# A row-sum kernel: both halves of a row summed at once in the last rows, loads of 9, 4 and 2 rows, and the first rows in two contiguous parts

**Chip and metric.** One core of a Trainium2 chip. The metric is the device time of one execution in microseconds (us); lower is better.

## The reference

```python
def setup_inputs():
    batch, seq, dim = 32, 512, 1024
    return {"x": np.random.randn(batch, seq, dim).astype(np.float32), "divisor": float(dim)}

def reference(x, divisor):
    return (np.sum(x, axis=-1) / divisor).astype(np.float32)
```

16384 rows of 1024 float32 are read (67.1 MB), 16384 numbers are written (64 KB). Each of the 128 partitions takes 128 rows.

## The kernel before

One queue (SP) issues every transfer. The first 16 rows of a partition lie in one part of the input, the other 112 in a second; each partition's results go out as 16, 96 and 16 neighbouring numbers, in three stores.

```python
F, L = 16, 16
M = J - F - L                      # 96
W = M + L                          # 112
x_first = bass.AP(tensor=x.tensor, offset=0, ap=[[F * D, P], [D, F], [1, D]])
... # x_main, x_last: pitch of W rows, behind x_first
o_first = bass.AP(tensor=out.tensor, offset=0, ap=[[F, P], [1, F]])      # 64 bytes a partition
o_main = bass.AP(tensor=out.tensor, offset=P * F, ap=[[W, P], [1, M]])
o_last = bass.AP(tensor=out.tensor, offset=P * F + M, ap=[[W, P], [1, L]])

first = [(2, 0), (14, 0)]          # (rows of a load, rows of it that ScalarE sums)
main = [(14, 0)] * 5 + [(14, 4), (12, 5)]
last = [(8, 4), (4, 2), (2, 1)]
...
    nc.vector.reduce_sum(out=dst[:, :d], in_=t[:, :d, :], axis=AX)       # VectorE's rows of a load
...
# the last two rows: one in a load of its own, one in three pieces pa, pb, pc
tc.keep_in_program_order(nc.sync.dma_start(out=o_first, in_=res0))       # behind the last load
tc.keep_in_program_order(nc.sync.dma_start(out=o_main, in_=res))
...
tc.keep_in_program_order(nc.sync.dma_start(out=o_last, in_=fin))
```

At the end of the program SP waits until every transfer but the last store has landed, and only then issues that last store (in the profile before, the others had landed by 157.87 and it was issued at 158.18). The kernel moves the store there itself:

```python
end.instructions = [
    with_sync(drain, on_wait=tuple(needs.values())),     # all earlier transfers landed
    with_sync(store, on_wait=(done,), on_update=(add,)), # then the store of fin
    *end.instructions[1:-1],
    with_sync(last, on_update=(sub,)),
]
```

Of the kernel before, what the change touches and what calls it, by code (L numbers as in the profile page):

```python
# [8 lines left out]

F32 = mybir.dt.float32  # L10
ADD = mybir.AluOpType.add
MULT = mybir.AluOpType.mult
COPY = mybir.ActivationFunctionType.Copy
AX = mybir.AxisListType.X
SP = mybir.EngineType.SP
# [52 lines left out]
def close_while_storing(nc, landed):  # L68


    body, end = nc.main_func.blocks[1], nc.main_func.blocks[-1]
    store = [i for i in body.instructions if i.engine == SP and type(i).__name__ == "InstDMACopy"][-1]
    (lane,) = store.sync_info.on_update
    drain = end.instructions[0]
    assert drain.engine == SP and type(drain).__name__ == "InstDrain"
    needs = {w.id: w for w in drain.sync_info.on_wait}
    assert needs[lane.id].wait_value > lane.update_value
    needs[lane.id] = dataclasses.replace(
        needs[lane.id], wait_value=needs[lane.id].wait_value - lane.update_value
    )  # L80

    (done,) = [w for w in store.sync_info.on_wait if w.ant_name.startswith("DVE_")]
    assert needs[done.id].wait_value == done.wait_value
    del needs[done.id]
    own = dict(sync_type="semaphore", id=landed.num, ant_name=landed.name)
    add = mybir.SyncUpdate(update_mode="sem-add-imm", update_value=16, **own)
    sub = mybir.SyncUpdate(update_mode="sem-sub-imm", update_value=16, **own)
    last = nc.sync.wait_ge(landed, 16).ins
    assert nc.main_func.blocks[-1].instructions[-1].name == last.name
    body.instructions = [i for i in body.instructions if i.name != store.name]  # L90
    end.instructions = [
        with_sync(drain, on_wait=tuple(needs.values())),
        with_sync(store, on_wait=(done,), on_update=(add,)),
        *end.instructions[1:-1],
        with_sync(last, on_update=(sub,)),
    ]


@with_exitstack
def kernel(  # L100
    ctx: ExitStack,
    tc: tile.TileContext,
    x: bass.AP,
    divisor: float,
    out: bass.AP,
):
    nc = tc.nc
    landed = nc.alloc_semaphore("landed")
    nc.at_finalize(start_loads_at_once)
    nc.at_finalize(latest_wait_first)  # L110
    nc.at_finalize(lambda nc: close_while_storing(nc, landed))
    xf = x.flatten_outer_dims()
    N, D = xf.shape
    P = nc.NUM_PARTITIONS
    scale = 1.0 / float(divisor)
    J = N // P
    assert J * P == N


    F, L = 16, 16  # L120
    M = J - F - L
    W = M + L
    x_first = bass.AP(tensor=x.tensor, offset=0, ap=[[F * D, P], [D, F], [1, D]])
    x_main = bass.AP(tensor=x.tensor, offset=P * F * D, ap=[[W * D, P], [D, M], [1, D]])
    x_last = bass.AP(tensor=x.tensor, offset=P * F * D + M * D, ap=[[W * D, P], [D, L], [1, D]])
    o_first = bass.AP(tensor=out.tensor, offset=0, ap=[[F, P], [1, F]])
    o_main = bass.AP(tensor=out.tensor, offset=P * F, ap=[[W, P], [1, M]])
    o_last = bass.AP(tensor=out.tensor, offset=P * F + M, ap=[[W, P], [1, L]])


    first = [(2, 0), (14, 0)]
    main = [(14, 0)] * 5 + [(14, 4), (12, 5)]
    last = [(8, 4), (4, 2), (2, 1)]
    assert sum(n for n, _ in first) == F
    assert sum(n for n, _ in main) == M and sum(n for n, _ in last) == L - 2
    bulk = ctx.enter_context(tc.tile_pool(name="bulk", bufs=3))
    one = ctx.enter_context(tc.tile_pool(name="one", bufs=1))
    psum = ctx.enter_context(tc.tile_pool(name="junk", bufs=4, space=bass.MemoryType.PSUM))

    res0 = one.tile([P, F], F32, name="res0")  # L140
    res = one.tile([P, M], F32, name="res")
    fin = one.tile([P, L], F32, name="fin")
    q = one.tile([P, L], F32, name="q")

    r = one.tile([P, 16], F32, name="r")[:, :1]

    def load(dst, src):
        tc.keep_in_program_order(nc.sync.dma_start(out=dst, in_=src))  # L148

    def act_sum(dst, src, by=1.0):  # L150
        n = src.shape[-1]
        junk = psum.tile([P, D], F32, name="junk")
        nc.scalar.activation(junk[:, :n], src, COPY, scale=by, accum_out=dst)  # L153

    def sums(dst, t, rows, on_act):
        d = rows - on_act
        for i in range(d, rows):
            act_sum(dst[:, i : i + 1], t[:, i, :])
        nc.vector.reduce_sum(out=dst[:, :d], in_=t[:, :d, :], axis=AX)  # L159

    for loads, src, dst in ((first, x_first, res0), (main, x_main, res)):
        j = 0
        for rows, on_act in loads:
            t = bulk.tile([P, 14, D], F32, name="t")
            load(t[:, :rows, :], src[:, j : j + rows, :])
            sums(dst[:, j : j + rows], t, rows, on_act)
            j += rows
        nc.gpsimd.tensor_scalar_mul(out=dst, in0=dst, scalar1=scale)  # L168
    j = 0
    for rows, on_act in last:  # L170
        if rows == 8:
            t = bulk.tile([P, 14, D], F32, name="t")[:, :8, :]
        else:
            t = one.tile([P, rows, D], F32, name=f"t{rows}")
        load(t, x_last[:, j : j + rows, :])
        sums(q[:, j : j + rows], t, rows, on_act)
        j += rows


    c = 704  # L180
    row = one.tile([P, D], F32, name="row")
    load(row, x_last[:, j, :])
    act_sum(r, row[:, c:], by=scale)
    nc.vector.reduce_sum(out=q[:, j : j + 1], in_=row[:, :c], axis=AX)  # L184



    a, b = 448, 704
    pa = one.tile([P, a], F32, name="pa")
    pb = one.tile([P, b - a], F32, name="pb")  # L190
    pc = one.tile([P, D - b + 2], F32, name="pc")
    load(pa, x_last[:, L - 1, :a])
    load(pb, x_last[:, L - 1, a:b])
    load(pc[:, : D - b], x_last[:, L - 1, b:])


    tc.keep_in_program_order(nc.sync.dma_start(out=o_first, in_=res0))
    tc.keep_in_program_order(nc.sync.dma_start(out=o_main, in_=res))

    act_sum(pc[:, D - b : D - b + 1], pa)  # L200
    nc.vector.reduce_sum(out=pc[:, D - b + 1 :], in_=pb, axis=AX)  # L201
    nc.gpsimd.tensor_scalar_mul(out=fin[:, :j], in0=q[:, :j], scalar1=scale)  # L202
    nc.gpsimd.tensor_scalar(  # L203
        out=fin[:, j : j + 1], in0=q[:, j : j + 1], scalar1=scale, scalar2=r, op0=MULT, op1=ADD
    )
    scaled = one.tile([P, D - b + 2], F32, name="scaled")
    nc.vector.tensor_scalar(  # L207
        out=scaled, in0=pc, scalar1=scale, scalar2=0.0, op0=MULT, op1=ADD, accum_out=fin[:, L - 1 :]
    )
    tc.keep_in_program_order(nc.sync.dma_start(out=o_last, in_=fin))  # L210


# [33 lines left out]
```

## Time and profile before

| | before |
|---|---|
| time, median of 5 runs | 161.13 us (160.92 to 161.52) |
| span of the profiled run | 159.6 us |
| VectorE busy | 120.9 us (76%) |
| DMA engines busy | 98.0% |
| last data landed / VectorE ended / last store issued | 157.54 / 158.15 / 158.18 us |

The kernel is bound by its stream of loads (the DMA engines are busy for 98.0% of the span, VectorE for 76%); the prediction shows the lines for that. The trace has 16 landing records, semaphore increments, for each of the 19 transfers, and a transfer is counted as landed at the last of them; a semaphore is the counter that others wait on. First the transfers of the results, with KB and the time from issue to landing, and then what SP waited for at the end (total, times, longest):

```profile
out_dram<-res SPq DMA_DIRECT2D x1, 48.0 KB, 10.1
out_dram<-res SPq DMA_DIRECT2D x1, 8.0 KB, 19.6
out_dram<-fin SPq DMA_DIRECT2D x1, 8.0 KB, 1.4
```
```profile
SPq L241 <- DMA out_dram<-res: 1.0, 1, 1.0
...
SPq L210 <- DVE scaled L207: 0.2, 1, 0.2
```

The first two stores were issued at 138.10 and 147.81 and landed at 157.70 and 157.87, just behind the last load (157.54). The line of 1.0 us covers the landing of the last pieces too. What SP waited for last was VectorE.

### The profile page before, as it was taken

Reading aid. Unit: us, or ns where it says so; the run is one execution under the profiler, and the core shown is the slowest. Engines: PE = TensorE matmul, PEld = TensorE weight load, DVE = VectorE, ACT = ScalarE, POOL = GpSimd, SP = SyncE. Lnnn points to the kernel's source line nnn. Section 1 sums busy time; section 2 is a strip of 40 time slices with the busy share of each in tenths; the row PEclk is TensorE's granted clock in tenths of the full one; section 3 lists DMA queues with packets and bytes.
Section 4 is the critical chain, followed back from the end, with each engine's and each line's share of the span. In section 5 each row is a group of like instructions: output and inputs, shape, how many; then the busy total and the mean of one; then the engine's idle time right before and its main releaser. Section 6 shows DMA issues by size and latency. Waiting matters only on the chain.

```text
span 159.6 us, 143 instructions
## 1 busy us (share of the span) xinstructions
DVE 120.9 (76%) x16; ACT 19.7 (12%) x37; POOL 1.4 (1%) x8
## 2 busy tenths in 40 slices
DVE  0500059995999599977999599959995996495985
ACT  3000000000000000000000000000000900490974
POOL 0000000000000000000000000000000000001001
DMA  7999999987999999978999999969999999898994
GB/s 253 470 460 460 460 460 460 431 374 345 460 460 460 460 460 460 417 345 388 460 460 460 460 460 460 402 302 445 460 460 427 394 431 542 357 443 378 413 407 133
DMA packets 2736, 67.18 MB, mean 421 GB/s; under 512 B 688, under 2 KB 1072, under 8 KB 1200
## 3 DMA queue, kind: packets, MB, share of 16 engines
q1 hardware_dynamic: 2736, 67.18, 98.0%
HBM read 67.11 MB, written 0.07 MB: 421 GB/s over the span
## 4 chain that ended last, share of the span: by engine, by line
DMA 76%; DVE 22%; SPq 0%; issue 0%; DVEq 0%
DMA t<-in_x_dram 76%; DVE res L159 20%; DVE q L159 1%; DVE q L184 1%; SPq L148 0%; DVE scaled L207 0%; DVE pc L201 0%; DVEq L207 0%; DVEq L241 0%
## 5 line engine op out<-in xcount | busy, mean ns | idle before, releaser
L159 DVE TENSOR_REDUCE res<-t 128x14 f32<-128x14336 f32 (+3 forms) x9 | 111.2, 12360 | 34.4 <-DMA t<-in_x_dram 34.4
L153 ACT ACTIVATE junk<-t 128x1024 f32<-128x1024 f32 x16 | 16.2, 1013 | 136.0 <-DMA t<-in_x_dram 136.0
L159 DVE TENSOR_REDUCE q<-t 128x4 f32<-128x4096 f32 (+2 forms) x3 | 7.9, 2642 | 2.7 <-DMA t<-in_x_dram 2.7
L153 ACT ACTIVATION_READ_ACCUMULATOR junk<-t 128x1 f32 x16 | 3.0, 187 | 0.0
L168 POOL TENSOR_SCALAR res<-res 128x16 f32<-128x16 f32 (+1 forms) x2 | 0.7, 352 | 145.1 <-DVE res L159 145.1
L153 ACT ACT_TABLE_LOAD x1 | 1.3, 1283 | 1.7 <-PEq L227 1.7
L184 DVE TENSOR_REDUCE q<-row 128x1 f32<-128x704 f32 x1 | 0.9, 885 | 0.0
L207 DVE TENSOR_SCALAR_CACHE_REDUCE scaled<-pc 128x322 f32<-128x322 f32 x1 | 0.5, 489 | 0.1
L153 ACT ACTIVATE junk<-pa 128x448 f32<-128x448 f32 x1 | 0.5, 547 | 0.0
L153 ACT ACTIVATE junk<-row 128x320 f32<-128x320 f32 x1 | 0.4, 442 | 0.1
L201 DVE TENSOR_REDUCE pc<-pb 128x1 f32<-128x256 f32 x1 | 0.4, 420 | 0.0
L202 POOL TENSOR_SCALAR fin<-q 128x14 f32<-128x14 f32 x1 | 0.3, 260 | 10.1 <-DVE q L159 10.1
L203 POOL TENSOR_SCALAR fin<-q,r 128x1 f32<-128x1 f32 x1 | 0.3, 265 | 0.7 <-DVE q L184 0.7
L153 ACT ACTIVATION_READ_ACCUMULATOR junk<-pa 128x1 f32 x1 | 0.2, 187 | 0.0
L153 ACT ACTIVATION_READ_ACCUMULATOR junk<-row 128x1 f32 x1 | 0.2, 186 | 0.0
L227 POOL MEMSET const-bfloat16-1.0<- 128x1 bf16 x1 | 0.1, 101 | 0.0
L227 POOL MEMSET const-uint8-127<- 128x1 uint8 x1 | 0.1, 101 | 0.0
L227 POOL MEMSET const-float32-0.0<- 128x1 f32 x1 | 0.1, 98 | 0.2 <-issue 0.2
L227 POOL MEMSET const-float32-1.0<- 128x1 f32 x1 | 0.1, 99 | 0.0
L207 DVE DVE_READ_ACCUMULATOR scaled<-pc 128x1 f32 x1 | 0.1, 82 | 0.0
## 6 DMA issues: line engine op xcount, KB each, us to landing
t<-in_x_dram SPq DMA_DIRECT2D x7, 7168.0 KB, 35.7
t<-in_x_dram SPq DMA_DIRECT2D x1, 6144.0 KB, 33.3
t<-in_x_dram SPq DMA_DIRECT2D x1, 4096.0 KB, 26.1
t<-in_x_dram SPq DMA_DIRECT2D x2, 1024.0 KB, 18.7
t<-in_x_dram SPq DMA_DIRECT2D x1, 2048.0 KB, 30.5
row<-in_x_dram SPq DMA_DIRECT2D x1, 512.0 KB, 33.2
pa<-in_x_dram SPq DMA_DIRECT2D x1, 224.0 KB, 33.3
pc<-in_x_dram SPq DMA_DIRECT2D x1, 160.0 KB, 33.0
```

The costliest lines, as they stand in the source:

```text
L153: nc.scalar.activation(junk[:, :n], src, COPY, scale=by, accum_out=dst)
L159: nc.vector.reduce_sum(out=dst[:, :d], in_=t[:, :d, :], axis=AX)
L168: nc.gpsimd.tensor_scalar_mul(out=dst, in0=dst, scalar1=scale)
L184: nc.vector.reduce_sum(out=q[:, j : j + 1], in_=row[:, :c], axis=AX)
L201: nc.vector.reduce_sum(out=pc[:, D - b + 1 :], in_=pb, axis=AX)
L202: nc.gpsimd.tensor_scalar_mul(out=fin[:, :j], in0=q[:, :j], scalar1=scale)
L203: nc.gpsimd.tensor_scalar(out=fin[:, j : j + 1], in0=q[:, j : j + 1], scalar1=scale, scalar2=r, op0=MULT, op1=ADD)
L207: nc.vector.tensor_scalar(out=scaled, in0=pc, scalar1=scale, scalar2=0.0, op0=MULT, op1=ADD, accum_out=fin[:, L - 1 :])
L227: nc = _bacc.Bacc("TRN2", target_bir_lowering=False, num_devices=1)
```

## The change

Its intent: start the stream on a contiguous megabyte; have fewer, larger loads at the end; and let VectorE sum a row of 1024 in 512 steps, by adding its two halves and accumulating the sums in the same instruction. The price is a third store of results ahead of the last one.

```diff
-    x_first = bass.AP(tensor=x.tensor, offset=0, ap=[[F * D, P], [D, F], [1, D]])
-    o_first = bass.AP(tensor=out.tensor, offset=0, ap=[[F, P], [1, F]])
+    E, F, L = 2, 14, 16
+    M = J - E - F - L
+    def part(row, pitch, n):
+        rows = bass.AP(tensor=x.tensor, offset=row * D, ap=[[pitch * D, P], [D, n], [1, D]])
+        return rows, bass.AP(tensor=out.tensor, offset=row, ap=[[pitch, P], [1, n]])
+    x_head, o_head = part(0, E, E)            # results: 8 bytes a partition
+    x_first, o_first = part(P * E, F, F)      # results: 56 bytes a partition
-    last = [(8, 4), (4, 2), (2, 1)]
+    last = [(9, 4), (4, 2), (2, 1)]
+    pad.tile([P, 224], F32, name="pad")
+    def dve_mean(dst, src, by=scale):
+        h = src.shape[-1] // 2
+        nc.vector.tensor_tensor_reduce(
+            out=src[:, :h], in0=src[:, :h], in1=src[:, h:], scale=by, scalar=0.0,
+            op0=ADD, op1=ADD, accum_out=dst,
+        )
... (VectorE's rows of the loads of 9, 4 and 2 go through dve_mean, one at a time, straight into fin)
... (the row in a load of its own, GpSimd's scaling of q, and ScalarE's part of the last row go)
-    load(pa, x_last[:, L - 1, :a])
-    load(pb, x_last[:, L - 1, a:b])
-    load(pc[:, : D - b], x_last[:, L - 1, b:])
+    load(pa, x_last[:, j, :c])                # c = 576
+    load(pb[:, : D - c], x_last[:, j, c:])
-    tc.keep_in_program_order(nc.sync.dma_start(out=o_first, in_=res0))
+    tc.keep_in_program_order(nc.sync.dma_start(out=o_head, in_=res_head))
+    tc.keep_in_program_order(nc.sync.dma_start(out=o_first, in_=res_first))
     tc.keep_in_program_order(nc.sync.dma_start(out=o_main, in_=res))
+    dve_mean(pb[:, D - c : D - c + 1], pa, by=1.0)
+    dve_mean(fin[:, j:], pb)
```

More of the change, by code (lines that the diff above doesn't have):

```diff
@@ L11 @@
 ADD = mybir.AluOpType.add
-MULT = mybir.AluOpType.mult
 COPY = mybir.ActivationFunctionType.Copy
@@ L117 @@
     assert J * P == N
-    F, L = 16, 16
-    M = J - F - L
-    W = M + L
-    x_first = bass.AP(tensor=x.tensor, offset=0, ap=[[F * D, P], [D, F], [1, D]])
-    x_main = bass.AP(tensor=x.tensor, offset=P * F * D, ap=[[W * D, P], [D, M], [1, D]])
-    x_last = bass.AP(tensor=x.tensor, offset=P * F * D + M * D, ap=[[W * D, P], [D, L], [1, D]])
-    o_first = bass.AP(tensor=out.tensor, offset=0, ap=[[F, P], [1, F]])
-    o_main = bass.AP(tensor=out.tensor, offset=P * F, ap=[[W, P], [1, M]])
-    o_last = bass.AP(tensor=out.tensor, offset=P * F + M, ap=[[W, P], [1, L]])
-    first = [(2, 0), (14, 0)]
+    E, F, L = 2, 14, 16
[5 more added lines that the diff above has]
+    x_first, o_first = part(P * E, F, F)
+    x_main, o_main = part(P * (E + F), M + L, M)
+    x_last, o_last = part(P * (E + F) + M, M + L, L)
+    head, first = [(E, 0)], [(F, 0)]
     main = [(14, 0)] * 5 + [(14, 4), (12, 5)]
-    last = [(8, 4), (4, 2), (2, 1)]
-    assert sum(n for n, _ in first) == F
-    assert sum(n for n, _ in main) == M and sum(n for n, _ in last) == L - 2
+    last = [(9, 4), (4, 2), (2, 1)]
+    assert sum(n for n, _ in main) == M and sum(n for n, _ in last) == L - 1
+    pad = ctx.enter_context(tc.tile_pool(name="pad", bufs=1))
+    pad.tile([P, 224], F32, name="pad")
     bulk = ctx.enter_context(tc.tile_pool(name="bulk", bufs=3))
@@ L138 @@
     psum = ctx.enter_context(tc.tile_pool(name="junk", bufs=4, space=bass.MemoryType.PSUM))
-    res0 = one.tile([P, F], F32, name="res0")
+    c = 576
+    t4 = one.tile([P, 4, D], F32, name="t4")
+    t2 = one.tile([P, 2, D], F32, name="t2")
+    pa = one.tile([P, 768], F32, name="pa")[:, :c]
+    pb = one.tile([P, D - c + 16], F32, name="pb")[:, : D - c + 2]
+    res_head = one.tile([P, 16], F32, name="res_head")[:, :E]
+    res_first = one.tile([P, 16], F32, name="res_first")[:, :F]
     res = one.tile([P, M], F32, name="res")
     fin = one.tile([P, L], F32, name="fin")
-    q = one.tile([P, L], F32, name="q")
-    r = one.tile([P, 16], F32, name="r")[:, :1]
+    nc.gpsimd.memset(pb[:, D - c :], 0.0)
     def load(dst, src):
@@ L150, in act_sum @@
     def act_sum(dst, src, by=1.0):
-        n = src.shape[-1]
         junk = psum.tile([P, D], F32, name="junk")
-        nc.scalar.activation(junk[:, :n], src, COPY, scale=by, accum_out=dst)
-    def sums(dst, t, rows, on_act):
-        d = rows - on_act
-        for i in range(d, rows):
-            act_sum(dst[:, i : i + 1], t[:, i, :])
-        nc.vector.reduce_sum(out=dst[:, :d], in_=t[:, :d, :], axis=AX)
-    for loads, src, dst in ((first, x_first, res0), (main, x_main, res)):
+        nc.scalar.activation(junk, src, COPY, scale=by, accum_out=dst)
+    def dve_mean(dst, src, by=scale):
[4 more added lines that the diff above has]
+        )
+    parts = ((head, x_head, res_head), (first, x_first, res_first), (main, x_main, res))
+    for loads, src, dst in parts:
         j = 0
@@ L165 @@
             load(t[:, :rows, :], src[:, j : j + rows, :])
-            sums(dst[:, j : j + rows], t, rows, on_act)
+            d = rows - on_act
+            for i in range(d, rows):
+                act_sum(dst[:, j + i : j + i + 1], t[:, i, :])
+            nc.vector.reduce_sum(out=dst[:, j : j + d], in_=t[:, :d, :], axis=AX)
             j += rows
@@ L170 @@
     for rows, on_act in last:
-        if rows == 8:
-            t = bulk.tile([P, 14, D], F32, name="t")[:, :8, :]
-        else:
-            t = one.tile([P, rows, D], F32, name=f"t{rows}")
+        t = bulk.tile([P, 14, D], F32, name="t")[:, :rows, :] if rows > 4 else t4 if rows == 4 else t2
         load(t, x_last[:, j : j + rows, :])
-        sums(q[:, j : j + rows], t, rows, on_act)
-        j += rows
-    c = 704
-    row = one.tile([P, D], F32, name="row")
-    load(row, x_last[:, j, :])
-    act_sum(r, row[:, c:], by=scale)
-    nc.vector.reduce_sum(out=q[:, j : j + 1], in_=row[:, :c], axis=AX)
-    a, b = 448, 704
-    pa = one.tile([P, a], F32, name="pa")
-    pb = one.tile([P, b - a], F32, name="pb")
-    pc = one.tile([P, D - b + 2], F32, name="pc")
-    load(pa, x_last[:, L - 1, :a])
-    load(pb, x_last[:, L - 1, a:b])
-    load(pc[:, : D - b], x_last[:, L - 1, b:])
-    tc.keep_in_program_order(nc.sync.dma_start(out=o_first, in_=res0))
-    tc.keep_in_program_order(nc.sync.dma_start(out=o_main, in_=res))
-    act_sum(pc[:, D - b : D - b + 1], pa)
-    nc.vector.reduce_sum(out=pc[:, D - b + 1 :], in_=pb, axis=AX)
-    nc.gpsimd.tensor_scalar_mul(out=fin[:, :j], in0=q[:, :j], scalar1=scale)
-    nc.gpsimd.tensor_scalar(
-        out=fin[:, j : j + 1], in0=q[:, j : j + 1], scalar1=scale, scalar2=r, op0=MULT, op1=ADD
-    )
-    scaled = one.tile([P, D - b + 2], F32, name="scaled")
-    nc.vector.tensor_scalar(
-        out=scaled, in0=pc, scalar1=scale, scalar2=0.0, op0=MULT, op1=ADD, accum_out=fin[:, L - 1 :]
-    )
+        d = rows - on_act
+        for i in range(rows):
+            if i < d:
+                dve_mean(fin[:, j + i : j + i + 1], t[:, i, :])
+            else:
+                act_sum(fin[:, j + i : j + i + 1], t[:, i, :], by=scale)
+        j += rows
+    load(pa, x_last[:, j, :c])
+    load(pb[:, : D - c], x_last[:, j, c:])
+    tc.keep_in_program_order(nc.sync.dma_start(out=o_head, in_=res_head))
+    tc.keep_in_program_order(nc.sync.dma_start(out=o_first, in_=res_first))
+    tc.keep_in_program_order(nc.sync.dma_start(out=o_main, in_=res))
+    dve_mean(pb[:, D - c : D - c + 1], pa, by=1.0)
+    dve_mean(fin[:, j:], pb)
     tc.keep_in_program_order(nc.sync.dma_start(out=o_last, in_=fin))
```

## The prediction

> **What bounds the kernel now.** I read the page first (its header, busy times and the chain that ended last), then the table of stretches, then the chain in order of time, then the groups by shape, and last the packet records.
>
> ```profile
> span 159.6 us, 143 instructions
> DVE 120.9 (76%) x16; ACT 19.7 (12%) x37; POOL 1.4 (1%) x8
> ...
> q1 hardware_dynamic: 2736, 67.18, 98.0%
> ...
> DMA 76%; DVE 22%; SPq 0%; issue 0%; DVEq 0%
> ```
>
> VectorE is busy for only 76% of the span. The one queue that carries all 67 MB fills the 16 DMA engines for 98% of it. The chain puts 22% on VectorE, but that is a way of drawing it: when a load landed at 38.83, VectorE had already been idle for 1.9 us. The same stretch can be put down to the transfers beside it.
>
> ```profile
> 0.00:5.00 5.00, 0.03 (x1) 1.28 (x1) 0.19 (x4) 1.00 1.03 393
> 5.00:22.00 17.00, 2.38 (x2) 0.00 (x0) 0.00 (x0) 1.00 1.00 432
> 22.00:138.00 116.00, 101.21 (x7) 4.27 (x8) 0.26 (x1) 1.00 0.99 431
> 138.00:157.60 19.60, 16.82 (x6) 14.12 (x28) 0.97 (x3) 1.00 0.96 404
> 157.60:159.60 2.00, 0.50 (x2) 0.00 (x0) 0.00 (x0) 1.00 0.05 4
> ```
>
> These are stretches of time; the last three columns are the granted clock, the busy share of the DMA engines, and GB/s. From 5 to 138 us the DMA engines are full at 431 to 432 GB/s. So only three things can move: the start (first packet at 1.02 us, first MB landed at 4.94 us), the small overheads of the short loads after 138, and the 2 us after the last data. The tail of the chain:
>
> ```profile
> 122.55 32.46 DMA t<-in_x_dram
> 155.01 0.02 issue
> 155.04 1.22 DVE q L159
> 156.25 0.01 issue
> 156.27 0.89 DVE q L184
> 157.15 0.39 DVE pc L201
> 157.55 0.04 DVEq L207
> 157.58 0.08 issue
> 157.66 0.49 DVE scaled L207
> ```
>
> By the landing records pc, the last piece of the last row, lands at 157.54, just when VectorE ends the sum of pb (157.55). Then 0.61 us of VectorE follow until 158.15; the last store is issued at 158.18, and the program ends 1.4 us later, at 159.6. What VectorE's operations cost:
>
> ```profile
> L159 DVE TENSOR_REDUCE res<-t 128x14 f32<-128x14336 f32 x6 | 90.5, 15086 | 23.9 <-DMA t<-in_x_dram 23.9
> L159 DVE TENSOR_REDUCE q<-t 128x1 f32<-128x1024 f32 x1 | 1.2, 1219 | 0.2 <-DMA t<-in_x_dram 0.2
> L207 DVE TENSOR_SCALAR_CACHE_REDUCE scaled<-pc 128x322 f32<-128x322 f32 x1 | 0.5, 489 | 0.1
> L207 DVE DVE_READ_ACCUMULATOR scaled<-pc 128x1 f32 x1 | 0.1, 82 | 0.0
> ```
>
> (15086 - 1219) / 13312 = 1.042 ns an element, and 1219 - 1024 x 1.042 = 152 ns fixed. The accumulating form fits the same line: 489 - 322 x 1.042 = 154 ns. Its accumulator read starts at 158.075, while the main instruction still runs, and ends 8 ns after it.
>
> [...] no two-input operation is in this trace. [...] The first two loads here have a pitch of 64 KiB; the 14-row one runs at 432 GB/s[...].
>
> **The change, part by part.** I keep the clock of the trace before and add the gain at the start at the end.
>
> *First rows.* Packets, bytes and loads stay; the pitch of the 2-row load falls from 64 to 8 KiB, that of the 14-row load from 64 to 56. By the packet records an 8 KiB packet takes 309 ns in the stream, 8 on each engine make 2.47 us, but the first load takes 3.53 us from its first packet (1.02) to its middle landing (4.55): about 0.3 us of landing, and some 0.7 us because the first 18 packets take 0.3 to 1.1 us each. I can't tell from the trace how much of that is a cold start and how much 16 streams 64 KiB apart. I choose a third: -0.25 us, anything from 0 to -0.5.
>
> *Loads of 9, 4, 2 and two pieces for the last row.* The row of its own goes into the 8-row load, and three pieces become two. In the records the eight last rows take 157.54 - 147.75 = 9.79 us; at the stream's 2118 / 14 x 8 = 1.210 us a row they would take 9.68, so only 0.11 us of overhead is there to be saved. Landings after: 9 rows 138.03 + 9.72 x 9/8 = 148.96; 4 rows + 4.82 = 153.78; 2 rows + 2.44 = 156.22; pa of 576 columns + 0.70 = 156.92 (2304-byte packets, interpolated between 74 ns at 1792 bytes and 159 at 4096, less the overlap the other pieces show); pb of 448 columns + 0.54 = 157.46. That is -0.08.
>
> *VectorE at the tail.* A half-and-half row: 152 + 512 x 1.042 = 686 ns, say 0.72 with its gap, against 1.07 for a row inside a long reduction. Five rows from 148.98 end at 152.6, before the 4 rows land (153.78); two end at 155.24, before the 2 rows land (156.22); one ends at 156.97. pa (288 steps, 0.45) ends at 157.45. pb carries the sum of pa as its 449th column (and a zero), so it waits for pa's accumulator; the same wait cost 0.11 before. It starts at 157.56 and ends at 157.96 (225 steps, 0.39 + 0.01). ACT ends its last row at 156.22 + 1.22 = 157.44. So all work is done at 157.96, against 158.15: -0.19. Both ScalarE's and GpSimd's work on the last row goes away, but none of it was on the path.
>
> *The third store.* The first two stores queue behind the last load and landed at 157.70 and 157.87, 0.16 us each after it. The last store is issued only when those have landed, and by the record the sequencer came out of that wait at about 158.0, 0.13 us after. With three: 157.46 + 3 x 0.16 + 0.15 = 158.09. This is later than the work (157.96), so the store's issue moves from 158.18 to 158.09 only: -0.09 of the -0.19.
>
> *Padding, memset.* Padding costs no time, and the rates above show nothing to repair; the memset runs on GpSimd at the start, off the path.
>
> Sum: -0.25 - 0.09 = -0.34, that is 161.13 - 0.34 = 160.8 us.
>
> **Rivals.** (a) Two fp32 inputs at half rate: a row costs 152 + 1067 + 30 = 1.25 us. Five end at 155.2, two more at 157.7, one at 159.0, pa 159.75, pb 160.5; the store goes out 2.35 us later and the time is 161.13 + 2.35 - 0.25 = 163.2. [...] against it [...] that the accumulating form in the trace pays nothing for its sum. I give it 1 in 10. (b) The start gains nothing, because the slow first packets are a cold start: 161.0. (c) The start gains all 0.7: 160.35. (d) The third store or the pa-pb wait costs 0.2 more than I think: 161.0.
>
> **Range and chances.** The three runs before spread over 0.45 us. (b) to (d) and that spread fill 160.3 to 161.3; (a) lies above. A gain of 2% would be 3.2 us, with 155 us of transfers untouchable (67.1 MB at 432 GB/s) and 1.0 us before the first packet, so it is all but excluded; a loss of 2% would be 164.4 us, more than even (a) makes.
>
> **What would show it.** The first load's landing should move from 4.94 to about 4.7, and the 14-row loads keep their period of 16.93 us (21.87 to 38.83 before). The new operation should take 0.69 us for 512 steps; 1.2 us means rival (a). VectorE should idle before the 4-row and 2-row loads, end about 0.5 us after pb lands, and SP should wait longest at the end for a store, not for VectorE. If the last landing moves by more than 0.1 us beyond what the first one moved, I have the overhead of the short loads wrong.

No term of the sum is cut: it still comes to -0.25 - 0.09 = -0.34, that is 160.8 us. Two of its grounds are estimates of mine. That the stream could not be made faster I took from the stretches with the DMA engines busy for 0.99 to 1.00 of the time at 431 to 432 GB/s. That the new operation, with its two inputs, would keep the 152 ns and 1.042 ns a step of the reductions was carried over from operations with one input. Rival (a), half that rate, was a supposition: the trace before shows nothing for it, and against it only that the accumulating form has 154 ns fixed where the reductions have 152.

## The result, and the profile after

The changed kernel took 163.35 us (median of 5, 163.17 to 163.75) against 161.13 before. The ratio is 1.0142, 95% interval 1.0122 to 1.0163. A ratio here is the mean time of one kernel's runs over that of the other's of the same rounds, so not quite the ratio of the medians. Within 2%, but slower where a small gain was predicted, and outside the range. First the page of the changed kernel and its table of stretches (two of five rows):

```profile
span 162.2 us, 150 instructions
...
DVE 117.3 (72%) x29; ACT 18.5 (11%) x33; POOL 1.2 (1%) x8
...
q1 hardware_dynamic: 2592, 67.18, 96.3%
```
```profile
138.00:157.40 19.40, 13.16 (x19) 12.81 (x24) 0.46 (x1) 1.00 0.96 405
157.40:162.20 4.80, 0.40 (x2) 0.00 (x0) 0.00 (x0) 1.00 0.02 2
```

Up to 157.4 us nothing is lost: the stretch from 138 moves 405 GB/s, against 404 before. What is new is the last row: 4.8 us in which the DMA engines are busy for 2% and VectorE for 0.4 us. The end of the chain, and the groups of the new operation:

```profile
123.39 34.00 DMA pb<-in_x_dram
157.39 0.04 issue
157.43 0.40 DVE pb L167
157.82 0.01 DVEq L236
```
```profile
L167 DVE CUSTOM_DVE_ANT_0 t<-t 128x512 f32<-128x512 f32 x8 | 5.1, 689 | 6.1 <-DMA t<-in_x_dram 6.1
...
L167 DVE CUSTOM_DVE_ANT_0 pb<-pb 128x225 f32<-128x225 f32 x1 | 0.4, 395 | 0.1
```

The last load landed at 157.39 and VectorE ended at 157.82, both earlier than before. The fused operation takes 689 ns for 512 steps. The chain follows the work back from its last instruction and so misses what came next. The timeline has it, and so have SP's waits and the transfers:

```profile
157.75 0.08 DVE L167 DVE_READ_ACCUMULATOR2_ANT fin<- 128x1 f32 x1
160.77 0.33 SPq L205 DMA_DIRECT2D out_dram<-fin  x1
```
```profile
SPq L236 <- DMA out_dram<-res: 3.2, 1, 3.2
```
```profile
out_dram<-res SPq DMA_DIRECT2D x1, 48.0 KB, 14.5
out_dram<-res_head SPq DMA_DIRECT2D x1, 1.0 KB, 35.6
out_dram<-res_first SPq DMA_DIRECT2D x1, 7.0 KB, 35.2
```

The last store was issued 2.9 us after all work was done. SP had waited 3.2 us for a store. The three (8, 56 and 384 bytes a partition) were issued at 123.88, 124.46 and 146.09, and landed at 159.44, 159.64 and 160.59 by the landing records, where two landed within 0.33 us of the last load before. Their packets (the pieces of a transfer in the profile's DMA records) were not long: those of 384 bytes took 22 ns each in both kernels, the 8-byte ones 9 ns, and the last of all of them ended at 157.27. So the late part lies between the end of a packet and its landing.

### The profile page after: what moved, and what is told of

Its sections match the earlier page's. It is cut to its first block, busy times and chain, and to the rows that moved or that the text cites. A ratio compares the mean times of both kernels' runs of the same rounds, so it can differ in the third digit from the quotient of the medians.

```text
span 162.2 us, 150 instructions
## 1 busy us (share of the span) xinstructions
DVE 117.3 (72%) x29; ACT 18.5 (11%) x33; POOL 1.2 (1%) x8
## 4 chain that ended last, share of the span: by engine, by line
DMA 76%; DVE 20%; SPq 1%; issue 0%; DVEq 0%
DMA t<-in_x_dram 55%; DMA pb<-in_x_dram 21%; DVE res L181 19%; DVE res_head L181 1%; SPq L157 1%; DVE pb L167 0%; DVEq L236 0%
## 5 line engine op out<-in xcount | busy, mean ns | idle before, releaser
L181 DVE TENSOR_REDUCE res<-t 128x14 f32<-128x14336 f32 (+2 forms) x7 | 93.9, 13411 | 14.8 <-DMA t<-in_x_dram 14.8
L181 DVE TENSOR_REDUCE res_first<-t 128x14 f32<-128x14336 f32 x1 | 15.1, 15085 | 14.6 <-DMA t<-in_x_dram 14.6
L167 DVE CUSTOM_DVE_ANT_0 t<-t 128x512 f32<-128x512 f32 x8 | 5.1, 689 | 6.1 <-DMA t<-in_x_dram 6.1
L181 DVE TENSOR_REDUCE res_head<-t 128x2 f32<-128x2048 f32 x1 | 2.3, 2287 | 4.9 <-DMA t<-in_x_dram 4.9
L183 POOL TENSOR_SCALAR res<-res 128x96 f32<-128x96 f32 x1 | 0.5, 458 | 108.4 <-DVE res L181 108.4
L167 DVE DVE_READ_ACCUMULATOR2_ANT fin<- 128x1 f32 x9 | 0.7, 83 | 0.0
L167 DVE CUSTOM_DVE_ANT_0 pa<-pa 128x288 f32<-128x288 f32 x1 | 0.5, 459 | 0.0
```

The costliest lines, as they stand in the source:

```text
L167: nc.vector.tensor_tensor_reduce(out=src[:, :h], in0=src[:, :h], in1=src[:, h:], scale=by, scalar=0.0, op0=ADD, op1=ADD, accum_out=dst,)
L181: nc.vector.reduce_sum(out=dst[:, j : j + d], in_=t[:, :d, :], axis=AX)
L183: nc.gpsimd.tensor_scalar_mul(out=dst, in0=dst, scalar1=scale)
```

## The experiments

The theory: the 8- and 56-byte stores land late, since several partitions write into the same 64 bytes of the result, and the last store waits for them. That sharing matters, and 64 bytes as its unit, was my assumption then; no run had shown it. Rivals: a third store as such; small pieces as such, whoever shares their 64 bytes; something else in the change (the fused operation, the last loads). The effects are read from the ratios and their 95% intervals.

### one_first: only the split undone

```diff
-    x_head, o_head = part(0, E, E)
-    x_first, o_first = part(P * E, F, F)
+    x_first, o_first = part(0, E + F, E + F)
-    head, first = [(E, 0)], [(F, 0)]
+    first = [(E, 0), (F, 0)]
-    tc.keep_in_program_order(nc.sync.dma_start(out=o_head, in_=res_head))
```

> The changed kernel with the first 16 rows of a partition in one part again (loads of 2 and 14 rows as in the kernel before, one store of 64 bytes a partition, two stores in all ahead of the last); everything else of the change stays. Theory (the small stores of 8 and 56 bytes land late and hold up the last store): the main result's store lands within 0.5 us of pb, the last store is issued about 0.05 to 0.2 us after VectorE ends, time 160.7 to 160.9, a ratio to before of 0.998. Rival (something else of the change holds the end, such as the fused operation or the last loads): time stays at 163.0 to 163.5.

160.69 us (160.64 to 160.90), ratio to before 0.9977 (0.9965 to 0.9989). As the theory had it: the rest of the change is a gain, if a small one, and this kernel is the fastest of the three, by 0.2% against the one before. In its timeline the last store follows VectorE at once, 0.03 us after its end at 157.86:

```profile
157.78 0.08 DVE L165 DVE_READ_ACCUMULATOR2_ANT fin<- 128x1 f32 x1
157.89 0.33 SPq L202 DMA_DIRECT2D out_dram<-fin  x1
```

### split_in_before: only the split done (edit shortened)

```diff
-    x_first, o_first   # 16 rows a partition, one store of 64 bytes
+    x_head, o_head     # 2 rows a partition, contiguous, a store of 8 bytes
+    x_first, o_first   # 14 rows a partition, contiguous, a store of 56 bytes
```

> The kernel before with one part of the change alone: the first 2 rows and the next 14 of each partition each in a contiguous part, with a third store. Theory: this alone brings the whole loss; the last store is issued some 3 us after the last load landed, time 163.2 to 163.9. Rival (the loss needs the other parts too): 161.0 to 161.3.

164.65 us (164.25 to 164.89), ratio 1.0210 (1.0191 to 1.0228): the split alone brings the loss, and more than I had expected: 3.5 us here, against 163.35 - 160.69 = 2.7 us in the changed kernel. In the profile the last of the three stores landed 3.28 us after the last load, against 3.20 in the changed kernel. The remaining difference, and the scatter of 0.55 to 0.69 us in the four kernels that pack the 8-byte pieces of all 128 partitions side by side, I leave open.

### three_whole: a third store, but whole

```diff
 # on one_first
-    ...dma_start(out=o_main, in_=res)
+    ...dma_start(out=o_main[:, : M // 2], in_=res[:, : M // 2])
+    ...dma_start(out=o_main[:, M // 2 :], in_=res[:, M // 2 :])
```

> As one_first, but the store of the main rows in two of 192 bytes a partition, so three stores stand ahead of the last one again, each in pieces that are multiples of 64 bytes and start at one. Theory: as one_first plus about 0.1 us for the landing of one more store, 160.8 to 161.0. Rival (the third store as such is the cost): 163.0 to 163.5.

160.93 us (160.84 to 161.16), ratio 0.9983 (0.9967 to 1.0000). Against one_first, whose before had the same median (161.15), the third store costs 0.2 us, not 2.7. The rival "a third store as such" falls.

### own_line: the same small pieces, but no partition shares its 64 bytes

```diff
-    x_head, o_head = part(0, E, E)
-    x_first, o_first = part(P * E, F, F)
+    x_head, o_head = part(0, E + F, E)
+    x_first, o_first = part(E, E + F, F)
```

> The changed kernel with three stores as there (8, 56 and 384 bytes a partition), but the first 2 and next 14 rows of a partition lie side by side as in the kernel before, so that each 64-byte piece of the result is written by one partition alone, in two pieces. Theory A (late because several partitions, on several DMA engines, write pieces of the same 64 bytes): lands early, 160.8 to 161.1. Theory B (late because a piece is smaller than 64 bytes, whoever else writes there): as the changed kernel, 163.0 to 163.5, or half of the loss.

161.09 us (median of 6; one at 161.97, the others 161.07 to 161.12), ratio 1.0007 (0.9991 to 1.0023). Three stores of 8, 56 and 384 bytes a partition, as in the changed kernel, yet most of the loss is gone. So smallness as such is not the cause of the loss of 2.7 us. Against one_first of the same rounds, 0.4 us are left, of which three_whole puts 0.2 on a third store; the rest may come from the two pieces, of two stores, that still lie in each 64 bytes. The profiled run is the one of 161.97, and its stream ran some 0.4 us later than in the other runs, so I rest this on the times.

### only_head8 and only_first56: which of the two stores

Each leaves one of the two small stores out, so their results are wrong.

```diff
 # only_head8
-    tc.keep_in_program_order(nc.sync.dma_start(out=o_first, in_=res_first))
 # only_first56
-    tc.keep_in_program_order(nc.sync.dma_start(out=o_head, in_=res_head))
```

> Wrong result on purpose: the changed kernel without the store of the next 14 rows (56 bytes a partition), with that of the first 2 (8 bytes a partition, 8 partitions in 64 bytes). It tells which of the two small stores is late. In the trace of the changed kernel the 8-byte store lands last at 159.44 and the 56-byte one at 159.64, 0.20 us later, so I expect most of the loss here: 162.2 to 163.3.

> Wrong result on purpose: the changed kernel without the store of the first 2 rows (8 bytes a partition), with that of the next 14 (56 bytes a partition, off the 64-byte grid, so that neighbours share 64 bytes in pairs). If sharing in pairs is as bad as sharing by eight: 162.2 to 163.3; if the 8-byte store makes the loss: 160.8 to 161.3.

163.02 us (162.73 to 163.42; ratio 1.0113, 1.0091 to 1.0134) with the 8-byte pieces, 160.94 (160.85 to 161.13; ratio 0.9983, 0.9969 to 0.9998) with the 56-byte ones. It is the 8-byte store. What SP waited for at the end, first in only_head8, then in only_first56:

```profile
SPq L235 <- DMA out_dram<-res_head: 2.7, 1, 2.7
SPq L235 <- DMA out_dram<-res: 0.3, 1, 0.3
```
```profile
SPq L235 <- DMA out_dram<-res_first: 0.3, 1, 0.3
SPq L235 <- DMA out_dram<-res: 0.2, 1, 0.2
```

### head8_every16, head8_every32, head8_every64: how many share

On only_head8, the 8-byte pieces are put further apart; results wrong.

```diff
+    o_head = bass.AP(tensor=out.tensor, offset=0, ap=[[4, P], [1, E]])   # 16 bytes; or 8 or 16 numbers: 32, 64 bytes
```

> Wrong result on purpose (two rows of the result are put elsewhere): as only_head8, but the 8-byte pieces lie 16 bytes apart, so 4 partitions share 64 bytes in place of 8. Theory A (the cost grows with the number of pieces in the same 64 bytes[...]): about half of only_head8's loss of 2.2 us, 161.8 to 162.2. Theory B (a cost of each piece below 64 bytes, however it lies): as only_head8, 162.7 to 163.4.

> Wrong result on purpose: as only_head8, pieces 32 bytes apart, 2 partitions to 64 bytes. Theory A: a quarter of the loss, 161.1 to 161.5. Theory B: 162.7 to 163.4. If what counts is 32 bytes and not 64, as head8_every64, within 0.15 us.

> Wrong result on purpose: as only_head8, pieces 64 bytes apart, none shares 64 bytes with another. Theory A: no loss or that of one piece, 160.8 to 161.1. Theory B: 162.7 to 163.4. If the loss stays and falls only for pieces further apart, what is shared is a larger block than 64 bytes.

| pieces in the same 64 bytes | time, us | ratio to before of the same rounds |
|---|---|---|
| 8 (only_head8) | 163.02 | 1.0113 (1.0091 to 1.0134) |
| 4 (head8_every16) | 161.65 | 1.0037 (1.0022 to 1.0052) |
| 2 (head8_every32) | 161.15 | 1.0005 (0.9990 to 1.0020) |
| 1 (head8_every64) | 160.87 | 0.9987 (0.9972 to 1.0002) |

The ratio falls with each step. (The first row was measured on another chip and in other rounds than the rest, so ratios are compared, not times.) Taken from the last row and times 161 us, the losses are 2.0, 0.8 and 0.3 us. That is close to 0.3 us for each further piece (7, 3 and 1 of them), so theory A was right in kind; it had put half of the loss, not three sevenths, at 4 pieces, and 161.65 lies under the expected 161.8. Theory B falls, and so does the thought that 32 bytes are what counts: from 32 to 64 bytes apart the time still fell by 0.28 us, and the two kernels' runs don't overlap (161.08 to 161.25 against 160.78 to 160.93). Pieces 64 bytes apart are fast (160.87 us) though 8 of them lie in 512 bytes, so no larger block is needed to explain the loss. But as the pieces moved apart, the area that they cover grew as well, from 1 KB to 8 KB, and no run has pieces further apart than 64 bytes or shifts them against a 64-byte border. What is shown is that pieces packed closer than 64 bytes apart cost time; that what they share is a block of 64 bytes is argued.

### head8_16parts: 16 pieces only

```diff
-    ...dma_start(out=o_head, in_=res_head)
+    ...dma_start(out=o_head[:16, :], in_=res_head[:16, :])
```

> Wrong result on purpose: as only_head8, but only partitions 0 to 15 are stored, 16 pieces of 8 bytes in 128 bytes: still 8 pieces in each 64 bytes, but of one piece for each DMA engine if the 16 partitions go to 16 engines. If pieces in the same 64 bytes delay each other whichever engine writes them: as only_head8, 162.7 to 163.4. If the delay comes from one engine writing the same 64 bytes several times: 160.8 to 161.2.

161.30 us (ratio 1.0004, 0.9984 to 1.0024), but scattered (160.81 to 161.65): between the two expectations. By the landing records 14 of the store's 16 increments came between 157.20 and 157.47, and two at 158.34 and 158.35. So some pieces in shared 64 bytes are late by 0.9 us here, but 8 pieces to 64 bytes do not always cost the 2.0 us of only_head8: here it is 0.3 us against head8_every64 by the ratios, 0.4 by the medians. The 0.3 us for each further piece holds only for stores of all 128 partitions; how many pieces there are in all (16 here), or how many of them one engine writes, may count too. Whether the delay needs one DMA engine to write the same 64 bytes several times this run doesn't settle, and the trace doesn't say which engine wrote which piece.

### early_small: the small stores in the middle

```diff
             load(t[:, :rows, :], src[:, j : j + rows, :])
+            if dst is res and j == 3 * 14:
+                tc.keep_in_program_order(nc.sync.dma_start(out=o_head, in_=res_head))
+                tc.keep_in_program_order(nc.sync.dma_start(out=o_first, in_=res_first))
```

> The changed kernel with the same three stores, but those of the first 2 and the next 14 rows issued in the middle of the program, behind the load of the fourth group of main rows, and not behind the last load. Theory (they land late and only hold up the end): late landings are hidden, time 160.6 to 160.9. Rival (the count of stores or bytes costs DMA time wherever they stand): the 14-row loads beside them take longer and the time stays above 162.

163.14 us (162.76 to 163.31), ratio 1.0120 (1.0105 to 1.0134): next to nothing is hidden. The half of my theory that said "they only hold up the end" fell. VectorE's timeline, first of the changed kernel, then of this one, with the idle time before each reduction in brackets:

```profile
106.41 15.09 DVE L181 TENSOR_REDUCE res<-t 128x14 f32<-128x14336 f32 x1 [1.83 <-DMA t<-in_x_dram]
```
```profile
89.53 15.09 DVE L184 TENSOR_REDUCE res<-t 128x14 f32<-128x14336 f32 x1 [1.79 <-DMA t<-in_x_dram]
108.86 15.09 DVE L184 TENSOR_REDUCE res<-t 128x14 f32<-128x14336 f32 x1 [4.25 <-DMA t<-in_x_dram]
125.74 10.82 DVE L184 TENSOR_REDUCE res<-t 128x10 f32<-128x10240 f32 x1 [1.79 <-DMA t<-in_x_dram]
```

The small stores follow the load that landed at 89.50 and landed at 91.96 and 92.13. The next load then came 2.4 us late, once (4.25 us of idle time against 1.83), and all later ones stayed late by as much. Those loads had been issued at 70.82 and 87.77, so the queue was not empty: the engines themselves lost the time. So these stores held up what was queued behind them here too, in the middle of the stream. The transfers landed in the order of the queue: in the changed kernel the 8-byte store first (159.44), then those of 56 and 384 bytes (159.64 and 160.59); here the 56-byte store (92.13) and a load (108.83) behind it. Why what stands behind it is late too no run shows. But the stream itself lost time, not the landings alone, as the packet records show: 25 packets of 56 KB that started between 89.0 and 93.1, right behind the small stores, took 2.5 to 4.4 us each. All others of that size here took less than 2.3 us, and in the changed kernel none took over 2.2 us.

### plain_sums: what the fused operation gives

```diff
 # on one_first, for VectorE's d rows of the loads of 9, 4 and 2
-                dve_mean(fin[:, j + i : j + i + 1], t[:, i, :])
+        nc.vector.reduce_sum(out=q[:, j : j + d], in_=t[:, :d, :], axis=AX)
+        nc.gpsimd.tensor_scalar_mul(out=fin[:, j : j + d], in0=q[:, j : j + d], scalar1=scale)
```

> As one_first, but VectorE's rows of the loads of 9, 4 and 2 are summed by one plain reduction a load and scaled by GpSimd, not by the fused operation; the last row keeps the fused operation. It tells what the fused operation gives. By the groups of before, a row costs 1.07 us in a long reduction against 0.61 us from start to start fused: 5 rows end at about 154.3, which is after the 4 rows land (153.6); those 2 rows end at 156.6, 1 row at 157.8, so pa and pb end about 1.0 us later than in one_first. Expected: time 0.8 to 1.1 us above one_first. If the fused operation gives nothing, the two are equal within 0.2 us.

161.41 us (161.30 to 161.55), ratio 1.0019 (1.0007 to 1.0031): 0.72 us above one_first, a little less than expected. Here VectorE is never idle from the landing of the 9 rows until pa:

```profile
148.63 8.80 DVE L193 TENSOR_REDUCE q<-t 128x5 f32<-128x5120 f32 x3 [3.23 <-DMA t<-in_x_dram]
157.35 0.45 DVE L166 CUSTOM_DVE_ANT_0 pa<-pa 128x288 f32<-128x288 f32 x1
```

So the merged load of 9 rows and the fused sums belong together: without the fused sums this arrangement is 0.2% slower than the kernel before, with them 0.2% faster.

## Why the prediction was wrong, point by point

- **The bound** was right. The stream ran at 431 to 432 GB/s in both kernels, and no part of the change touched it.
- **First rows: wrong.** I gave the contiguous start -0.25 us. The first load landed at 4.88 us, against 4.94 before, and over all profiles the nine kernels with the contiguous 2 rows had a mean of 4.85 us, the five with the 64 KiB pitch 4.78. Rival (b) holds in its number: nothing is gained. Its reason, a cold start, no run shows.
- **Loads of 9, 4 and 2: right.** pb was put at 157.46, less what the start gave; it landed at 157.39.
- **VectorE at the tail: right in kind, a little better in size.** 686 ns a row were predicted, 689 measured; from start to start it is 0.61 us, not 0.72, as the next instruction starts before the one ahead has ended (starts at 148.79, 149.41 and 150.02, each of 0.69 us). VectorE ended at 157.82.
- **The third store: the step that failed.** The prediction gave "157.46 + 3 x 0.16 + 0.15 = 158.09" for the issue of the last store, and took 0.16 us a store from stores of 64 and 384 bytes. Measured: the stores landed 3.20 us after pb in place of 0.48, and the last store was issued at 160.77. This term is short by 2.7 us. In the profiled run, which was the slowest of the five (163.75), the whole miss is 2.9 us, and the rest of it is the start; by the medians the miss is 2.55 (163.35 against 160.8). I named the wait as the one that would bind, and its sign, that SP waits longest for a store, came true, but through landings that I had not foreseen. I gave it 0.2 us more as rival (d), but never asked how the 8-byte pieces lie in the result: 8 partitions in the same 64 bytes. One_first, only_head8 and the row of pitches show that pieces packed this closely are what costs; own_line and three_whole that neither small pieces nor a third store do it alone.
- **Rival (a)** came to 163.2 us, near the measured time, and is wrong all the same: the two-input operation, with float32 inputs and an accumulator, took 689 ns for 512 steps and 395 for 225, so 1.02 ns a step, against 1.042 an element in the plain reduction. A time alone does not confirm a cause.
- **Open:** what makes closely packed pieces land late, and why what stands behind them in the queue waits too, whether 64 bytes is the unit that they share, whether it matters which engine writes them or how many there are, and why the split cost 0.8 us more in the kernel before than in the changed one.

## What to carry to other kernels

In these runs a store counted by where its pieces lay, not by its bytes: 1 KB in pieces of 8 bytes, 8 of them in the same 64 bytes, cost 2.0 us (only_head8, 163.02 us), and the same pieces 64 bytes apart nothing that showed (head8_every64, 160.87 us). What stood behind the packed ones in the queue waited too, loads included (2.4 us in early_small). So try to give each partition's piece of a result its own 64 bytes: a rearrangement of the input also rearranges the results, and the stores can cost more than the loads gain (here 2.7 us, and nothing gained at the start). And when the chain ends well before the program does, look at what the issuing queue waited for: the missing time was not in the chain, and that view named a store, for 3.2 us.
